# One plain feature tile fewer in the second up product of a macaron layer: three plain tiles instead of four

## The chip, the cores and the metric

The kernel runs on one core of one Trainium2 chip. The metric is the device time of one execution in microseconds (us), lower is better. Engines are named as the profile names them: PE (TensorE, matrix products), PEld (its weight loads), DVE (VectorE), ACT (ScalarE), POOL (GpSimd), SP (SyncE, which issues most transfers; its queue is SPq).

## The reference

One layer on 512 tokens of 1024 channels, in float32:

```
x = x + 0.5 * swiglu_ffn(rmsnorm(x, ffn1_norm), w_gate1, w_up1, w_down1)
x = x + hybrid_mixer(rmsnorm(x, mix_norm), w_in, ...)
x = x + 0.5 * swiglu_ffn(rmsnorm(x, ffn2_norm), w_gate2, w_up2, w_down2)
x = rmsnorm(x, final_norm)
swiglu_ffn(x, g, u, d) = (silu(x @ g) * (x @ u)) @ d      # hidden width 2816
```

The mixer is an attention over eight heads beside a pooling mixer. The change touches the third line alone, and in it the two products `x @ g` and `x @ u`.

## The kernel before, in words

**Numbers.** Every float32 operand of a product is split into a high part that PE can take (`hi`, made by ACT with a copy that rounds) and the rest (`lo`, made by DVE with a subtraction). A product then is three matrix instructions: high by high, high by low, low by high. `mm3` issues them, on lines 187, 188 and 189.

**The up product** (`ffn_up`, called once for each of the two feed-forward blocks). The 2816 hidden features are 22 tiles of 128. A tile needs its gate and its up column block, each 1024 x 128, against the 512 tokens. A tile is computed in one of two ways.

- *Plain*: 2 blocks x 8 pieces of the contraction x 3 instructions = 48 matrix instructions of 128x512. Weights: two transfers `raw<-in_wA_dram` (line 180), each split by ACT (L131, CAST) and DVE (L132).
- *Seven products*: contraction, tokens, and the pair gate/up are each halved, and the 2x2x2 block product is made with seven half-size products instead of eight (a Strassen-Winograd scheme). That is 7 x 4 pieces x 3 = 84 matrix instructions of 128x256. The order of the seven, by the activation operand: A11, S3, S2, A22, S1, A12, S4. Weights of the seven come as four parts: `11` (one block, 512 columns), `13` and `24` (sums made by DVE on lines 489, 495, 496) and `22`. ACT rounds each (L466), DVE makes the low part (L471). Below, "the low part of 24" is the L471 row that writes `parts<-wsum` with the 24 sum; product 3 (S2) is the first that reads it.

`PLAIN` gives the number of plain tiles of each block. With the second block's value of 4, the stage runs in this order:

1. Tiles 0 and 1 together, "the first group": 96 instructions into four accumulators (`first`). The norm of the tokens is finished in the middle of it, and only then is its row `rb` known.
2. Plain tiles 2 to plain - 2, each with its two blocks one after the other (line 514). For 4, this is tile 2.
3. Plain tile plain - 1, "the transition tile" (line 526), its two blocks interleaved piece by piece, so that the 16 normalized token buffers (`h`) come free one pair after another. Here ACT and DVE put the halved operands of the token side into those buffers (`ha`), and the first weights of the seven products are made.
4. Tiles plain to 21 by seven products (line 570), the order of PE, DVE and ACT written out by hand.

The token side of the seven products is a list of 19 steps, `norm.blocks` (line 337): eight scalings by the norm (L354), four sums of 128x1024 (L360), and seven splits: `xa` twice (S3 and S2, L134/L135), `sa` (S4), and four of two halves each, `ha` (A11, A22, S1, A12). The list `todo` holds them; `piece(n)` issues the next n:

```
for n, f in enumerate(down.order[2 : plain - 1], 2):     # 514
    for j in range(2):
        ... piece(4)                                     # 522
    down.make_sums(evacuate(f, *banks))
piece(len(todo) - 4)                                     # 524
...
for k in range(KD):                                      # 530, transition tile
    ... k == 1, 3, 5: piece()
high24(plain); low24(plain)                              # 546
down.make_sums(evacuate(f, *banks))
piece()
```

A plain tile is finished by `evacuate`: DVE multiplies the gate by `rb` (L413), ACT takes silu (L415), DVE multiplies again (L417) and multiplies with the up accumulator (L716); every second tile adds two short sums (L723, L724). In steps 1 to 3 a scheduler of the program's own decides the order on PE, DVE and ACT when the program is built; only SP keeps the written order. All engines then work through their own list in order.

Accumulators rotate through four `mm` banks and four `a` banks. Weight parts rotate through four places (three in `parts`, one in `whi`/`wlo`). `make_sums` lets POOL start the sums of the down weights; one call belongs to each tile from 2 on.

Of the kernel before, what the change touches and what calls it, by code (L numbers as in the profile page):

```python
# [34 lines left out]
RAW = 2  # L35
HILO = 3
SHIFT = 16
PLAIN = (5, 4)
PROBS = 3
EARLY = 8  # L40

# [14 lines left out]
def layer(  # L56
# [140 lines left out]
    def residual_tiles():  # L197
        pairs = [xpool.tile([P, 2 * S], F32, tag=f"x{k}", name=name("x")) for k in range(KD // 2)]
        x_pairs[:] = pairs
        return [pairs[k // 2][:, k % 2 * S : (k % 2 + 1) * S] for k in range(KD)]  # L200
# [651 lines left out]
    with tc.tile_pool(name="act1", bufs=1, reuse_waits="tile") as apool, ExitStack() as in_order:  # L852
        down1.begin(apool)
        ffn_up(n1, wA1, down1, False, in_order, PLAIN[0])
        x[:] = residual_tiles()
# [891 lines left out]
    with tc.tile_pool(name="act2", bufs=1, reuse_waits="tile") as apool, ExitStack() as in_order:  # L1747
        down2.begin(apool)

        ffn_up(n3, wA2, down2, True, in_order, PLAIN[1], (6, 7))  # L1750
        xt, gb = [None] * (2 * NT), [None] * 2
# [243 lines left out]
```

## Time and profile before

| what | value |
|---|---|
| median of 3 runs | 831.91 us (831.65 to 832.68) |
| the profiled execution's own time | 833.59 us |
| its span in the trace | 831.5 us |
| PE busy | 819.8 us (99%) |
| DVE busy | 715.0 us (86%) |
| ACT busy | 499.9 us (60%) |
| POOL busy | 147.2 us (18%) |

In a row of the timeline the columns are start, duration (us), engine, line, operation, output<-input, shape, count, and in square brackets the time the engine sat idle before it and what ended that. A PE row's duration overlaps the next row, so the pace of PE is read from the distance of two starts. Durations of DVE and ACT rows overlap the next by some 0.1 us too. A windows row gives, for a stretch, its length and the busy time of each engine.

### The profile page before, as it was taken

Reading aid. Unit: us, or ns where it says so; the run is one execution under the profiler, and the core shown is the slowest. Engines: PE = TensorE matmul, PEld = TensorE weight load, DVE = VectorE, ACT = ScalarE, POOL = GpSimd, SP = SyncE. Lnnn points to the kernel's source line nnn. Section 1 sums busy time; section 2 is a strip of 40 time slices with the busy share of each in tenths; the row PEclk is TensorE's granted clock in tenths of the full one; section 3 lists DMA queues with packets and bytes.
Section 4 is the critical chain, followed back from the end, with each engine's and each line's share of the span. In section 5 each row is a group of like instructions: output and inputs, shape, how many; then the busy total and the mean of one; then the engine's idle time right before and its main releaser. Section 6 shows DMA issues by size and latency. Waiting matters only on the chain.

```text
span 831.5 us, 15009 instructions
## 1 busy us (share of the span) xinstructions
PE 819.8 (99%) x5730; PEld 755.6 (91%) x5730; DVE 715.0 (86%) x1123; ACT 499.9 (60%) x854; POOL 147.2 (18%) x234
## 2 busy tenths in 40 slices
PE   9999999999999999999999999999999999999996
PEld 7889999999999999878878888899999999988885
DVE  7899999899987987678699688989999999977896
ACT  8346555666656665549659545465665555756573
POOL 0023212222310000334033063111111011100010
PEclk9999999999999999999999999999999999999998
DMA  8266989879998674999411267255666576859632
GB/s 282 73 203 204 239 221 260 205 198 235 253 303 280 194 225 140 240 308 242 173 52 52 82 156 213 68 108 204 160 181 158 148 206 158 275 195 317 202 115 102
DMA packets 73704, 158.56 MB, mean 191 GB/s; under 512 B 6545, under 2 KB 31649, under 8 KB 73249
## 3 DMA queue, kind: packets, MB, share of 16 engines
q1 hardware_dynamic: 49664, 109.09, 39.0%
q0 software_dynamic: 23680, 48.24, 27.6%
q8 instruction: 45, 0.74, 0.4%
q10 hardware_dynamic: 288, 0.27, 0.1%
q14 instruction: 27, 0.21, 0.1%
HBM read 153.38 MB, written 50.34 MB: 245 GB/s over the span
## 4 chain that ended last, share of the span: by engine, by line
PE 94%; DVE 2%; DMA 2%; ACT 1%; issue 0%; SPq 0%; DVEq 0%; ACTq 0%
PE mm L187 21%; PE mm L189 21%; PE mm L188 21%; PE a L187 9%; PE a L188 9%; PE a L189 9%; DMA raw<-in_wQK_dram 1%; PE a L1588 1%; DMA raw<-in_wA_dram 1%; PE mm L1499 1%; PE mm L1563 1%; PE a L1563 0%; PE mm L1588 0%; DVE t L1332 0%; DVE parts L1109 0%
## 5 line engine op out<-in xcount | busy, mean ns | idle before, releaser
L131 ACT CAST parts<-raw 128x1024 fp32r<-128x1024 f32 (+2 forms) x77 | 74.0, 969 | 63.0 <-PE mm L188 27.2
L560 ACT ACTIVATE t<-mm 128x256 f32<-128x256 f32 x105 | 40.3, 384 | 115.3 <-PE mm L189 112.5
L132 DVE TENSOR_TENSOR parts<-raw,parts 128x1024 fp32r<-128x1024 f32 (+2 forms) x77 | 85.7, 1121 | 20.7 <-ACT parts L131 17.5
L187 PE MATMUL mm<-ha,parts 128*128 128x256 f32 x280 | 77.4, 277 | 0.0
L189 PE MATMUL mm<-ha,parts 128*128 128x256 f32 x280 | 77.4, 277 | 0.0
L188 PE MATMUL mm<-ha,parts 128*128 128x256 f32 x280 | 77.4, 276 | 0.0
L706 POOL DMA_DIRECT2D wsum<-in_wB_dram x72 | 71.5, 1167 | 28.1 <-DMA wsum<-wsum 14.5
L704 POOL COPY mark<-t 128x1 f32<-128x1 f32 x40 | 16.1, 402 | 338.2 <-DVE t L604 249.7
L471 DVE TENSOR_TENSOR parts<-wsum,parts 128x1024 fp32r<-128x1024 f32 x53 | 64.6, 1219 | 5.8 <-PE mm L189 4.0
L466 ACT CAST parts<-wsum 128x1024 fp32r<-128x1024 f32 x53 | 53.9, 1049 | 0.4 <-DVE wsum L496 0.2
L187 PE MATMUL mm<-hhi,parts 128*128 128x512 f32 x136 | 53.3, 396 | 0.6 <-ACT parts L131 0.5
L189 PE MATMUL mm<-hhi,parts 128*128 128x512 f32 x136 | 53.2, 394 | 0.0
L188 PE MATMUL mm<-hlo,parts 128*128 128x512 f32 x136 | 52.9, 390 | 0.0
L187 PEld LDWEIGHTS mm<-ha,parts 128*128 128x128 f32 x280 | 52.6, 188 | 0.1
L188 PEld LDWEIGHTS mm<-ha,parts 128*128 128x128 f32 x280 | 52.6, 188 | 0.1
L189 PEld LDWEIGHTS mm<-ha,parts 128*128 128x128 f32 x280 | 52.6, 188 | 0.0
L132 DVE TENSOR_TENSOR ah<-acts,ah 128x512 fp32r<-128x512 f32 (+1 forms) x72 | 47.2, 663 | 5.1 <-ACT ah L131 5.1
L131 ACT CAST ah<-acts 128x512 fp32r<-128x512 f32 (+1 forms) x72 | 40.9, 580 | 9.9 <-PE mm L188 7.6
L471 DVE TENSOR_TENSOR parts<-raw,parts 128x512 fp32r<-128x512 f32 (+1 forms) x52 | 43.5, 860 | 0.0
L489 DVE TENSOR_TENSOR wsum<-raw 128x1024 f32<-128x1024 f32 x35 | 42.7, 1219 | 0.0
L1109 DVE TENSOR_TENSOR parts<-raw,parts 128x1024 fp32r<-128x1024 f32 x24 | 30.3, 1266 | 12.8 <-ACT parts L1104 12.7
L466 ACT CAST parts<-raw 128x512 fp32r<-128x512 f32 (+1 forms) x52 | 39.3, 755 | 2.0 <-DMA raw<-in_wA_dram 1.4
(340 smaller groups left out, 3050.4 us busy)
## 6 DMA issues: line engine op xcount, KB each, us to landing
raw<-in_wA_dram SPq DMA_DIRECT2D x87, 512.0 KB, 4.9
wsum<-in_wB_dram POOLq DMA_DIRECT2D x60, 512.0 KB, 7.7
raw<-wsum SPq DMA_DIRECT2D x36, 512.0 KB, 4.7
raw<-in_wB_dram SPq DMA_DIRECT2D x30, 512.0 KB, 5.1
wsum<-wsum POOLq DMA_DIRECT2D x20, 512.0 KB, 5.3
x<-in_xT_dram SPq DMA_DIRECT2D x16, 256.0 KB, 9.0
raw<-in_wQK_dram SPq DMA_DIRECT2D x8, 512.0 KB, 5.7
wsum<-in_wB_dram POOLq DMA_DIRECT2D x12, 256.0 KB, 6.2
```

The lines of the kernel that those rows point to most:

```text
L131: nc.scalar.copy(hi, src)
L132: nc.vector.tensor_tensor(lo, src, hi.bitcast(F32), op=ALU.subtract)
L187: nc.tensor.matmul(acc, a[0], b[0], start=start, stop=False, **more)
L188: nc.tensor.matmul(acc, a[0], b[1], start=False, stop=False, **more)
L189: nc.tensor.matmul(acc, a[1], b[0], start=False, stop=stop, **more)
L466: nc.scalar.copy(hi, src)
L471: nc.vector.tensor_tensor(lo, src, hi.bitcast(F32), op=ALU.subtract)
L489: nc.vector.tensor_tensor(z, raw[:, : 2 * S], raw[:, S : 3 * S], op=ALU.add)
L560: nc.scalar.activation(dst, src, AF.Copy, scale=scale)
L704: nc.gpsimd.tensor_copy(mark[:, 0:1], after[:, 0:1])
L706: nc.gpsimd.dma_start(self.rows(i, g), self.rows(self.terms[i][at], g), **(dict(accum_op=ALU.add) if at else {}),)
L1109: nc.vector.tensor_tensor(lo, buf["raw", i], hi.bitcast(F32), op=ALU.subtract)
```

## The change

The number of plain tiles of the second up product goes from 4 to 3:

```
-PLAIN = (5, 4)
+PLAIN = (5, 3)
```

`ffn_up` is called with `plain = 3`. The loop on line 514 is empty; tile 2 becomes the transition tile, and tile 3 is made of seven products. `piece(len(todo) - 4)` now issues 15 of the 19 steps right after the first group, where it used to find 11 left and issued 7. In the rows below names carry their buffer numbers: `aside` is the room of scaled tokens and their sums, `raw` a weight as it came, `wsum` a sum of weights.

On DVE, at the end of the first group (difference of the two orders; `raw_6269` and `raw_6302` are the weights of the old tile 2, `raw_6363` the first of the old transition tile, `raw_6293` and `raw_6297` those of the new one):

```order
-L132 TENSOR_TENSOR parts<-raw_6269,parts 128x1024
 L354 SCALAR_TENSOR_TENSOR aside_6264<-x_2854,gain_sb,rb_6212 128x512 x2
 L354 SCALAR_TENSOR_TENSOR aside_6264<-x_2855,gain_sb,rb_6212 128x512 x2
-L132 TENSOR_TENSOR parts<-raw_6302,parts 128x1024
 L354 SCALAR_TENSOR_TENSOR aside_6265<-x_2856,gain_sb,rb_6212 128x512 x2
 L354 SCALAR_TENSOR_TENSOR aside_6265<-x_2857,gain_sb,rb_6212 128x512 x2
+L132 TENSOR_TENSOR parts<-raw_6293,parts 128x1024
 L360 TENSOR_TENSOR aside_6266<-aside_6264,aside_6265 128x1024
-L132 TENSOR_TENSOR parts<-raw_6363,parts 128x1024
+L132 TENSOR_TENSOR parts<-raw_6297,parts 128x1024
 L360 TENSOR_TENSOR aside_6264<-aside_6266,aside_6264 128x1024
```

All eight scalings now stand together, and behind them both weight splits are already those of the transition tile.

On DVE, around the low part of 24, before (`wsum_6439` is the 24 sum, `mm_6373` and `mm_6374` the accumulators of the transition tile):

```order
L132 TENSOR_TENSOR ha_6479<-aside_6265,ha_6478 128x512
L413 TENSOR_TENSOR t_6464<-mm_6373,rb_6212 128x512
L471 TENSOR_TENSOR parts<-wsum_6439,parts 128x1024
L417 TENSOR_TENSOR t_6466<-t_6466,rb_6212 128x512
L132 TENSOR_TENSOR ha_6483<-aside_6265,ha_6482 128x512
L716 TENSOR_TENSOR acts_6093<-mm_6374,t_6466 128x2x256
```

and in the changed kernel (`wsum_6369` is the 24 sum, `wlo_6346` the low part of 13, `mm_6301` and `mm_6302` the accumulators):

```order
L471 TENSOR_TENSOR wlo_6346<-wsum_6343,whi_6345 128x1024
L496 TENSOR_TENSOR wsum_6369<-wsum_6369,raw_6303 128x512
L132 TENSOR_TENSOR ha_6373<-aside_6266,ha_6372 128x512
L413 TENSOR_TENSOR t_6394<-mm_6301,rb_6212 128x512
L132 TENSOR_TENSOR ha_6377<-aside_6266,ha_6376 128x512
L471 TENSOR_TENSOR parts<-wsum_6369,parts 128x1024
L417 TENSOR_TENSOR t_6396<-t_6396,rb_6212 128x512
L132 TENSOR_TENSOR ha_6407<-aside_6265,ha_6406 128x512
L716 TENSOR_TENSOR acts_6093<-mm_6302,t_6396 128x2x256
```

Two of the eight `ha` rows stand behind the low part of 24 instead of one, and the low part of 13 has moved close ahead of it.

On ACT, the rounding of the weights for the first tile of seven products, in the changed kernel (`parts<-raw_6303` is 22, `parts<-wsum_6369` is 24; the L560 row copies the sum of product 1 out of its accumulator):

```order
L466 CAST whi_6345<-wsum_6343 128x1024
L131 CAST ha_6372<-aside_6266 128x512
L466 CAST parts<-raw_6303 128x1024
L131 CAST ha_6376<-aside_6266 128x512
L466 CAST parts<-wsum_6369 128x1024
L415 ACTIVATE t_6396<-t_6394 128x512
L131 CAST ha_6406<-aside_6265 128x512
L560 ACTIVATE t_6422<-mm_6419 128x256
```

Before, 24 stood ahead of 22 in this list; now 22 is ahead, and behind 24 come the silu of the transition tile, one more `ha`, and then the copy.

On PE, at the start of the transition tile, in the changed kernel (`mm_6301` is its gate accumulator, `mm_6302` its up accumulator, in the bank that held the up block of tile 0):

```order
L189 MATMUL mm_6301<-hhi_5902,parts 128x512
L187 MATMUL mm_6301<-hhi_5916,parts 128x512
L188 MATMUL mm_6301<-hlo_5917,parts 128x512
L189 MATMUL mm_6301<-hhi_5916,parts 128x512
L187 MATMUL mm_6302<-hhi_5887,parts 128x512
L188 MATMUL mm_6302<-hlo_5888,parts 128x512
```

The scheduler put the gate's first three pieces (nine instructions) ahead of the up block's first; the code alternates them one piece at a time.

## The prediction

> **What bounds the kernel now.** I read the page first: how much of the chain that ended last is PE.
>
> ```profile
> span 831.5 us, 15009 instructions
> ...
> PE 94%; DVE 2%; DMA 2%; ACT 1%; issue 0%; SPq 0%; DVEq 0%; ACTq 0%
> ```
>
> PE is the end's chain nearly everywhere, so a PE instruction less is time less, as long as the operands of the next ones are there. That is a question of the stage, so I read the stage in windows: plain tile 2, the transition tile, the first tile of seven products, and the 17 that follow.
>
> ```profile
> 524.34:535.22 10.88, 10.88 (x49) 9.02 (x49) 10.88 (x16) 4.61 (x7) 1.68 (x1) 1.00 0.00 1
> 535.22:546.10 10.88, 10.88 (x49) 9.02 (x48) 8.77 (x13) 5.85 (x9) 1.99 (x2) 1.00 0.42 122
> 546.10:555.72 9.62, 9.62 (x85) 9.62 (x84) 9.55 (x15) 6.19 (x12) 1.99 (x4) 1.00 0.52 112
> ...
> 555.72:717.50 161.78, 161.78 (x1430) 161.78 (x1429) 149.65 (x211) 96.44 (x175) 22.05 (x39) 1.00 0.65 181
> ```
>
> The first busy number is PE, the third DVE, the fourth ACT. PE is busy all through, at full clock (1.00). A plain tile takes 10.88 us, a tile of seven products 161.78 / 17 = 9.52 us, the first of them 9.62. But DVE is busy through all of plain tile 2 (10.88 of 10.88) and through nearly all of the first product tile (9.55 of 9.62). Later DVE needs 149.65 / 17 = 8.80 us of each 9.52. **So PE sets the time, and DVE, which makes the operands, is only just ahead of it at the place where the change works.**
>
> **What the change removes from PE.** The pace of PE, from the distance of starts:
>
> ```profile
> 524.34 0.39 PE L187 MATMUL mm<-hhi,parts 128*128 128x512 f32 x1
> 524.57 0.39 PE L188 MATMUL mm<-hlo,parts 128*128 128x512 f32 x1
> ...
> 526.38 0.39 PE L187 MATMUL mm<-hhi,parts 128*128 128x512 f32 x1
> ...
> 546.10 0.28 PE L187 MATMUL mm<-ha,parts 128*128 128x256 f32 x1
> 546.22 0.28 PE L188 MATMUL mm<-ha,parts 128*128 128x256 f32 x1
> ...
> 548.84 0.35 PE L187 MATMUL mm<-xa,parts 128*128 128x256 f32 x1
> 549.03 0.28 PE L188 MATMUL mm<-xa,parts 128*128 128x256 f32 x1
> ```
>
> A 128x512 instruction takes (526.38 - 524.34) / 9 = 0.227 us; 48 of them are 10.88. A 128x256 one takes 9.52 / 84 = 0.113; 84 are 9.52. The gain on PE is 1.36 us. The first product tile lost 0.10 us, most of it at 548.84, where product 3 waited; counted apart, since that tile is replaced too: 1.36 + 0.10 = **1.46 us to gain, if PE never waits**. That is 0.18% of the time: small, so waits decide.
>
> The Trainium skill ("TensorE: Matmul & The Clock Gate", section on the back-to-back issue gap) says that in a real kernel the spacing is set by the matrix product and the weight load together, and gives 81 ns at 128 columns and 131 ns at 512. As an estimate from that page, 48 x 131 ns = 6.3 us against 84 x (81 to 131) ns = 6.8 to 11.0 us would make the smaller products the dearer ones by 0.5 to 4.7 us. The starts quoted above do not agree: 227 ns and 113 ns, in proportion to the columns.
>
> **What the change takes away as cover.** Plain tile 2 gave DVE 10.88 us while PE needed little from it. In the changed kernel PE starts the transition tile at 524.34 and the first product tile at 535.22 instead of 546.10. DVE loses with tile 2 only two weight splits and one tile's evacuation; the 19 token steps stay. So I add up DVE's list up to the low part of 24, in the changed order, with durations of this trace as distances of starts:
>
> ```profile
> 509.99 0.59 ACT L331 COPY rb<-a 128x512 f32<-128x512 f32 x1 [0.48 <-PE a L329]
> ...
> 511.47 2.73 DVE L354 SCALAR_TENSOR_TENSOR aside<-x,gain_sb,rb 128x512 f32<-128x512 f32 x4
> 514.52 1.23 DVE L132 TENSOR_TENSOR parts<-raw,parts 128x1024 fp32r<-128x1024 f32 x1 [0.31 <-ACT parts L131]
> 515.66 2.73 DVE L354 SCALAR_TENSOR_TENSOR aside<-x,gain_sb,rb 128x512 f32<-128x512 f32 x4
> ...
> 521.11 1.22 DVE L360 TENSOR_TENSOR aside<-aside,aside 128x1024 f32<-128x1024 f32 x1
> 522.24 1.22 DVE L360 TENSOR_TENSOR aside<-aside 128x1024 f32<-128x1024 f32 x1
> 523.38 0.69 DVE L413 TENSOR_TENSOR t<-mm,rb 128x512 f32<-128x512 f32 x1
> 523.98 1.22 DVE L135 SCALAR_TENSOR_TENSOR xa<-aside,xa 128x1024 fp32r<-128x1024 f32 x1
> ...
> 530.98 0.42 DVE L723 TENSOR_TENSOR acts<-acts 128x256 f32<-128x256 f32 x1
> 531.32 1.22 DVE L132 TENSOR_TENSOR sa<-aside,sa 128x1024 fp32r<-128x1024 f32 x1
> ...
> 546.58 1.22 DVE L471 TENSOR_TENSOR parts<-wsum,parts 128x1024 fp32r<-128x1024 f32 x1
> ```
>
> The prices: a scaling 0.66 (four last 2.73 and the last alone about 0.75), a step of 1024 elements 1.14 (514.52 to 515.66; 1.13 from 521.11 to 522.24), a step of 512 elements 0.60 (523.38 to 523.98), a short sum 0.34 (530.98 to 531.32). DVE can start when `rb` is there, 509.99 + 0.59 = 510.6. Then stand, in the changed order:
>
> - eight scalings, 5.3; two weight splits, 2.3; four sums, 4.5: 12.1 us, to 522.7;
> - two `xa` and one `sa`, 3.4; the evacuation of tiles 0 and 1, six times 0.60 and two short sums, 4.3: to 530.4;
> - low part of 11, 0.6; the sums of 13 and 24, 1.14 + 0.6 + 0.6; low part of 13, 1.14: 4.1, to 534.5;
> - six `ha` halves, 3.6, and the first multiplication of the transition tile's evacuation, 0.6: to 538.7.
>
> So the low part of 24 runs from 538.7 and, with its 1.22, ends at **539.95**. I see no row in this list for which DVE would have to stand still: each input is ready some tenths before its turn. PE wants the part in the third instruction of product 3: 535.22 + 26 x 0.113 = 538.2. **PE waits there 1.8 us.** It was not so before: there the row started at 546.58 and was done at 547.80, one us ahead of product 3.
>
> ACT says the same by another way. Product 3 adds to the accumulator of product 1, so ACT must have copied product 1 out first (L560). Its rows before:
>
> ```profile
> 545.44 1.05 ACT L466 CAST parts<-wsum 128x1024 fp32r<-128x1024 f32 x1
> 546.39 0.62 ACT L131 CAST ha<-aside 128x512 fp32r<-128x512 f32 x1
> 546.91 0.63 ACT L415 ACTIVATE t<-t 128x512 f32<-128x512 f32 x1
> ...
> 548.38 0.37 ACT L560 ACTIVATE t<-mm 128x256 f32<-128x256 f32 x1
> ```
>
> The copy ended at 548.75 and product 3 began its wait-free run right after, at 548.84. Now the rounding of 22 stands ahead of that of 24. It needs the place that the transition tile's up block leaves at its end, 535.3; 0.95 for it, 0.52 for an `ha`, 0.95 for 24 bring ACT to 537.7; the silu waits for DVE's 538.1 row and ends its turn near 538.75, one more `ha` 0.5, the copy 0.37: 539.7. Product 3 would start at 539.7 instead of 537.94, **1.75 us late**. The two waits lie beside each other, so they cost 1.8 us once, not twice.
>
> **The next tiles.** DVE is behind now, and its list goes on. Further prices of the hand-written order:
>
> ```profile
> 551.92 1.22 DVE L489 TENSOR_TENSOR wsum<-raw 128x1024 f32<-128x1024 f32 x1
> 553.17 0.69 DVE L495 TENSOR_TENSOR wsum<-wsum,raw 128x512 f32<-128x512 f32 x1
> 553.90 0.69 DVE L496 TENSOR_TENSOR wsum<-wsum,raw 128x512 f32<-128x512 f32 x1
> 554.51 0.42 DVE L604 TENSOR_TENSOR t<-a,t 128x256 f32<-128x256 f32 x1
> ```
>
> From the start of the low part of 24 (538.7): itself 1.14, four rows of 0.60, 22's low part 1.14, 11's 0.60, the sums 1.25 + 0.73 + 0.61, two short rows 0.68 make 8.55, so the second tile's low part of 13 starts at 547.3 and ends at 548.5. PE begins that tile at 535.22 + 9.52 + 1.8 = 546.5 and wants the part 14 instructions later, at 548.1: a wait of 0.4. The low part of 24 then ends at 547.3 + 1.14 + 0.34 + 1.22 = 549.97, wanted at 549.9: 0.1. In the third tile the same sum gives the part of 13 at 557.5, wanted at 558.15; from there DVE's 0.7 us of air in each tile keeps it ahead.
>
> **The start of the transition tile** is at the edge too. Its up accumulator takes the bank of tile 0's up block, which DVE frees with an L716 row; by the list above that row starts at 525.7 and ends near 526.4. PE has nine gate instructions first and wants the bank at 526.38 (the third start quoted for PE). I count 0.05 us. The weights themselves are ready by 519.5, by the same list.
>
> **What is only moved.** The transfers of the first seven-product weights go out earlier; each takes 2.9 to 7.2 us and has more than that before its use. POOL's calls for the down sums stay 20, one a tile. The four places of the weight parts change roles by two, in the same cycle. I count nothing for these, with some tenths either way as the range.
>
> ```profile
> L180 SPq DMA_DIRECT2D raw<-in_wA_dram x21: 327/328/524, 1.2 to 509.8; - x21
> ...
> DMA to landing us min/median/max: 2.9/4.2/7.2
> ```
>
> **The sum.** Gained 1.46; lost 0.05 + 1.8 + 0.4 + 0.1 = 2.35, less rounding 2.3. Net **+0.8 us**. Against its own execution (833.59, the span of 831.5 and 2.1 around it) that is 834.4; that execution stood 1.7 above the median of 831.91, so the forecast against the median is **832.7 us**, +0.1%. A measurement of this kernel tells about 0.2%, 1.7 us, from no change.
>
> **The rivals.**
>
> Of the first rival the profile has one row to weigh, DVE's `ha` rows of the old kernel from 511.47 to 547.9:
>
> ```profile
> L132 DVE TENSOR_TENSOR ha<-aside,ha 128x512 fp32r<-128x512 f32 x7 | 4.8, 689 | 2.1 <-ACT ha L131 1.3 <-PE mm L188 0.7
> ```
>
> - *No wait appears.* If the low part of 24 were issued by 537.0 and the copy of product 1 done by 537.9, the whole 1.46 would stay: 830.45. For it: DVE does have idle slots in the old transition tile (8.77 of 10.88), so its list is not always tight. Against it: those slots (2.1 us) are waits for `ha`, whose room PE frees piece by piece, and the sum above holds no slot to squeeze; 1.75 us would have to be wrong in it. Chance 0.09. It stays inside 0.2%.
> - *The evacuation comes late at the start of the transition tile, and nothing takes that back.* Place: the up block's first instruction, at 526.38. The price is one for one, since ACT's chain to the copy of product 1 starts from the end of the transition tile: it keeps its 1.75 us however late that end is. The point from which it decides is 0.85 us: from there the total is 0.8 + 0.85 = 1.65, slower by 0.2%. What could do it: on ACT the rounding of 11 now stands ahead of the `xa` roundings. It waits for a transfer sent about 509.8 behind the others, landing by 517.0 if it takes the longest 7.2, and ACT is wanted for `xa` from 520.6. So 3.6 us of margin speak against it; small delays of 0.02 us in each of DVE's 40 rows speak for it. Typical result +2.3: 834.2. Chance 0.13.
> - *Half-size products are paced by their weight loads.* At 0.227 us for each of 84, the tile would be 19.0 us, and the time 831.91 + 8.2 + 0.8 = 840.9. The product tiles of this trace run at 0.113. Chance 0.01.
> - *The change does not do what it says.* The order shows 36 more PE instructions, 84 - 48. Excluded.
>
> **How the numbers follow.** Forecast 0.77, its own range 831.5 to 833.7: 0.8 us from delays that I did not see, as much from overlaps that I did not count, and the spread of the three runs. The no-wait case ends at 830.45, the late case about 834.2. Leaving out less than 2 in 10: 831.0 to 834.2. Faster than 830.25 needs more than the whole gain: 0.02. Slower than 833.55 is most of the late case and the upper edge of the forecast: 0.16. Within: 0.82.
>
> **What would show it.** In the changed profile: PE's idle time before product 3's third instruction (or its first) in the first product tile, 1.7 to 1.9 us, released by DVE L471 or ACT L560; 0.3 to 0.5 in the second tile at the low part of 13; nothing from the fourth tile on, which then runs at 9.52; DVE without idle time from 510.6 to 540. Wrong would be: PE's wait at another place, above all at 526.4 or 535.2, or waits past the third tile, or a changed pace in the down product behind.

## The result, and the profile after

The changed kernel takes **833.64 us** (median of 20 runs, 832.29 to 837.03). The kernel before, run beside it, takes 832.59 (20 runs, 831.62 to 834.31). The ratio is **1.0016, 95% interval 1.0009 to 1.0022**: about a microsecond slower. The forecast was +0.8 us: 832.7 against 831.91, the median of three runs that was known then. With twenty runs that median is 832.59, so it is the difference that is to be compared, +1.05 us.

The page of the changed kernel:

```profile
span 835.0 us, 15097 instructions
...
PE 820.9 (98%) x5766; PEld 757.8 (91%) x5766; DVE 719.0 (86%) x1129; ACT 503.1 (60%) x861; POOL 145.1 (17%) x234
...
PE 85%; DVE 6%; DMA 5%; issue 2%; ACT 1%; SPq 1%; DVEq 0%; ACTq 0%
```

The span is 3.5 us longer than before, more than the medians say; the profiled execution, 837.03 us, is the slowest of the twenty. So the first question is where in the span the difference lies. I cut it by starts of PE rows. The **stretch** below runs from the first product of the second block (`hhi,parts`) to the first instruction of the down product behind it (`parts,ah`). It holds all that the change touches.

| | before | after |
|---|---|---|
| first product of the second block | 500.77 | 503.35 |
| its plain part, to the first 128x256 instruction | 45.33 | 34.44 |
| its seven-product part, to the first down product | 171.46 | 183.28 |
| **stretch** | **216.79** | **217.72** |
| down product, to the last row of PE | 105.68 | 105.69 |

The stretch costs **+0.93 us**. Behind it nothing changed. The 2.58 us ahead of it lie in code that is the same in both kernels; the last experiment shows what they are. Rows of the changed kernel are therefore 2.57 or 2.58 us late against those of before, and "on the clock of before" means with 2.57 taken off.

The stretch in windows, cut at the first instruction of each tile: transition tile, first and second tile of seven products, third, and the rest (length, then busy time and rows of PE, PEld, DVE, ACT, POOL, then the granted clock of PE):

```profile
526.91:537.79 10.88, 10.88 (x49) 9.01 (x48) 10.88 (x18) 4.78 (x8) 0.00 (x0) 1.00 0.01 4
537.79:549.26 11.47, 9.91 (x85) 9.71 (x84) 11.40 (x17) 7.17 (x12) 1.40 (x2) 1.00 0.32 55
549.26:559.23 9.97, 9.92 (x87) 9.72 (x86) 9.87 (x16) 6.41 (x11) 1.62 (x4) 1.00 0.89 225
559.23:568.75 9.52, 9.52 (x87) 9.52 (x86) 9.01 (x13) 5.74 (x12) 1.78 (x3) 1.00 0.77 185
568.75:721.07 152.32, 152.32 (x1347) 152.32 (x1345) 140.75 (x200) 90.55 (x164) 20.41 (x36) 1.00 0.65 177
```

PE is idle in two of these rows only: it works 9.91 of 11.47 us in the first product tile, 9.92 of 9.97 in the second. A PE row lasts longer than its pace, so busy time hides short waits; the lengths show them. Against the 9.52 us of every later tile the first lost 1.95 and the second 0.45, together 2.40 us. DVE, the third busy number, is full in the transition tile and all but full in the first product tile. The gaps themselves, in the timeline of PE:

```profile
540.42 0.28 PE L189 MATMUL a<-xa,wlo 128*128 128x256 f32 x1
542.25 0.38 PE L187 MATMUL mm<-xa,parts 128*128 128x256 f32 x1 [1.56 <-ACT t L560]
...
550.74 0.28 PE L188 MATMUL a<-xa,whi 128*128 128x256 f32 x1
551.07 0.39 PE L189 MATMUL a<-xa,wlo 128*128 128x256 f32 x1
```

At a pace of 0.113 from start to start, product 3 of the first product tile begins 1.72 us late, and two instructions close behind lose 0.11 and 0.06 more. In the second tile the low part of 13 costs 0.22 + 0.11, product 3 another 0.06. That is 2.28 of the 2.40 us; the rest are starts a little wider apart than 0.113, and no other gap in the stretch is new.

What DVE did there, with no idle time in brackets on any row:

```profile
538.86 0.68 DVE L496 TENSOR_TENSOR wsum<-wsum,raw 128x512 f32<-128x512 f32 x1
539.47 0.68 DVE L132 TENSOR_TENSOR ha<-aside,ha 128x512 fp32r<-128x512 f32 x1
540.07 0.68 DVE L413 TENSOR_TENSOR t<-mm,rb 128x512 f32<-128x512 f32 x1
540.67 0.68 DVE L132 TENSOR_TENSOR ha<-aside,ha 128x512 fp32r<-128x512 f32 x1
541.27 1.21 DVE L471 TENSOR_TENSOR parts<-wsum,parts 128x1024 fp32r<-128x1024 f32 x1
```

and ACT:

```profile
539.58 1.05 ACT L466 CAST parts<-wsum 128x1024 fp32r<-128x1024 f32 x1 [0.20 <-DVE wsum L496]
540.78 0.63 ACT L415 ACTIVATE t<-t 128x512 f32<-128x512 f32 x1 [0.15 <-DVE t L413]
541.32 0.60 ACT L131 CAST ha<-aside 128x512 fp32r<-128x512 f32 x1
541.83 0.37 ACT L560 ACTIVATE t<-mm 128x256 f32<-128x256 f32 x1
```

The low part of 24 starts at 541.27, on the clock of before at 538.70, and is there at 542.48. The copy of product 1 is done at 542.20, and PE goes on at 542.25. The trace names the copy, but ACT itself waits for DVE twice on the way to it (L496, L413). That is still a reading of one trace: the copy alone, the order on ACT, or DVE's list could each be the cause, and they end within 0.3 us of each other. The experiments take them apart.

### The profile page after: what moved, and what is told of

Its sections match the earlier page's. It is cut to its first block, busy times and chain, and to the rows that moved or that the text cites. A ratio compares the mean times of both kernels' runs of the same rounds, so it can differ in the third digit from the quotient of the medians.

```text
span 835.0 us, 15097 instructions
## 1 busy us (share of the span) xinstructions
PE 820.9 (98%) x5766; PEld 757.8 (91%) x5766; DVE 719.0 (86%) x1129; ACT 503.1 (60%) x861; POOL 145.1 (17%) x234
## 4 chain that ended last, share of the span: by engine, by line
PE 85%; DVE 6%; DMA 5%; issue 2%; ACT 1%; SPq 1%; DVEq 0%; ACTq 0%
PE mm L187 19%; PE mm L188 18%; PE mm L189 18%; PE a L187 9%; PE a L188 9%; PE a L189 9%; DMA raw<-in_wQK_dram 2%; DMA t<-ext_d 1%; DMA raw<-in_wV_dram 1%; DVE parts L1109 1%; PE a L1588 1%; DMA raw<-in_wA_dram 1%; PE mm L1499 1%; PE mm L1563 1%; DVE aside L354 1%
## 5 line engine op out<-in xcount | busy, mean ns | idle before, releaser
L560 ACT ACTIVATE t<-mm 128x256 f32<-128x256 f32 x108 | 41.5, 384 | 117.6 <-PE mm L189 114.6
L131 ACT CAST parts<-raw 128x1024 fp32r<-128x1024 f32 (+2 forms) x74 | 70.9, 967 | 56.6 <-PE mm L188 23.0
L132 DVE TENSOR_TENSOR parts<-raw,parts 128x1024 fp32r<-128x1024 f32 (+2 forms) x74 | 82.1, 1116 | 15.7 <-ACT parts L131 15.1
L187 PE MATMUL mm<-ha,parts 128*128 128x256 f32 x288 | 79.5, 276 | 0.0
L189 PE MATMUL mm<-ha,parts 128*128 128x256 f32 x288 | 79.5, 276 | 0.0
L188 PE MATMUL mm<-ha,parts 128*128 128x256 f32 x288 | 79.5, 276 | 0.0
L471 DVE TENSOR_TENSOR parts<-raw,parts 128x512 fp32r<-128x512 f32 x72 | 65.8, 950 | 0.6 <-ACT parts L466 0.6
L466 ACT CAST parts<-raw 128x512 fp32r<-128x512 f32 x72 | 59.7, 829 | 5.2 <-DMA raw<-in_wA_dram 2.5
L187 PEld LDWEIGHTS mm<-ha,parts 128*128 128x128 f32 x288 | 54.1, 188 | 0.1
L188 PEld LDWEIGHTS mm<-ha,parts 128*128 128x128 f32 x288 | 54.1, 188 | 0.1
L189 PEld LDWEIGHTS mm<-ha,parts 128*128 128x128 f32 x288 | 54.1, 188 | 0.0
L471 DVE TENSOR_TENSOR wlo<-wsum,whi 128x1024 fp32r<-128x1024 f32 x36 | 44.1, 1224 | 10.3 <-PE mm L189 7.9
L187 PE MATMUL mm<-hhi,parts 128*128 128x512 f32 x128 | 50.6, 400 | 0.2 <-ACT parts L131 0.2
L189 PE MATMUL mm<-hhi,parts 128*128 128x512 f32 x128 | 50.0, 394 | 0.0
L188 PE MATMUL mm<-hlo,parts 128*128 128x512 f32 x128 | 49.7, 390 | 0.0
L471 DVE TENSOR_TENSOR parts<-wsum,parts 128x1024 fp32r<-128x1024 f32 x36 | 43.7, 1215 | 0.0
```

The source lines that it names most:

```text
L131: nc.scalar.copy(hi, src)
L132: nc.vector.tensor_tensor(lo, src, hi.bitcast(F32), op=ALU.subtract)
L187: nc.tensor.matmul(acc, a[0], b[0], start=start, stop=False, **more)
L188: nc.tensor.matmul(acc, a[0], b[1], start=False, stop=False, **more)
L189: nc.tensor.matmul(acc, a[1], b[0], start=False, stop=stop, **more)
L466: nc.scalar.copy(hi, src)
```

## The experiments

The theory is that of the prediction: DVE's list decides when product 3 may go. The rivals are ACT's copy, and ACT's order (22 rounded ahead of 24). Every kernel is the changed one with the edit shown.

**One: the copy no longer matters (e1).** Products 3, 5 and 7 of the first product tile go to an empty bank; product 1 is thereby left out of that tile's later sums.

```
-                product(acc, cut(w24, 0, S), S2, False)
+                acc = abank()[:, :HT] if n == plain == 3 else acc; product(acc, cut(w24, 0, S), S2, n == plain == 3)
```

> Changed kernel, but in the first tile of seven products (tile 3 of the second block) products 3, 5 and 7 are summed in a spare bank that begins empty, so that product 3 need not wait for ACT's copy of product 1 (L560). Left out of the computation: product 1 in the sums behind it, for this one tile. The list of DVE is the same. Theory (DVE is behind; its low part of 24 ends 2.5 us after product 3 could start): PE's wait stays, 1.6 to 1.8 us, and moves from the first to the third instruction of product 3, released by DVE L471; the stretch from the first hhi product of the second block to its first down product stays 217.7 us within 0.15. Rival (ACT's copy alone holds PE, 24 is ready earlier): the wait falls under 0.5 us and the stretch to 216.5 or less.

Measured: 832.62 us in one run, stretch 217.82. PE's timeline, then DVE's:

```profile
538.01 0.39 PE L189 MATMUL a<-xa,parts 128*128 128x256 f32 x1 [1.36 <-DVE parts L471]
```

```profile
536.73 1.23 DVE L471 TENSOR_TENSOR parts<-wsum,parts 128x1024 fp32r<-128x1024 f32 x1
```

The wait moved by two instructions, to the first that reads the low part of 24, and kept its size (1.52 beyond the pace there). The stretch stayed. Taking the copy away gains nothing, since DVE's row is as late as the copy. So the copy alone is not the cause.

**Two: 22 rounded behind the copy (e6).**

```
-                high(n, (n, 22), raws[n][:, 2 * S :])
-                low((n, 22))
-                w22 = w[n, 22][:2]
+                first3 = n == plain == 3
+                if not first3: high(n, (n, 22), raws[n][:, 2 * S :]); low((n, 22))
...
+                if first3: high(n, (n, 22), raws[n][:, 2 * S :]); low((n, 22))
+                w22 = w[n, 22][:2]
```

> Changed kernel, but ACT's rounding of 22 for the first product tile stands behind the copy of product 1 instead of ahead of the rounding of 24; 24 is ahead of 22 as in the kernel before. DVE's list is unchanged up to the low part of 24. Theory (DVE's list sets it; silu, and with it the copy behind it, wait for DVE's L413 row): PE's wait at product 3 stays 1.6 to 1.8 us, the stretch stays 217.7 within 0.15 us. Rival (the turned order of ACT made the wait): copy and 24 are ready 0.9 us earlier and the wait falls to 0.9 us or less, stretch 216.9 or less.

Measured: 833.96 us in one run, stretch 218.09. ACT, then PE:

```profile
536.11 1.05 ACT L466 CAST parts<-wsum 128x1024 fp32r<-128x1024 f32 x1 [1.48 <-DVE wsum L496]
...
538.28 0.38 ACT L560 ACTIVATE t<-mm 128x256 f32<-128x256 f32 x1
```

```profile
538.71 0.39 PE L187 MATMUL mm<-xa,parts 128*128 128x256 f32 x1 [1.57 <-ACT t L560]
...
540.97 0.39 PE L187 MATMUL a<-ha,parts 128*128 128x256 f32 x1 [0.57 <-ACT t L560]
```

With 22 out of the way ACT stands idle 1.48 us for DVE's 24 sum, and product 3 is 1.73 us late, as before. ACT's order is not the cause. I missed one thing: the second copy, which product 4 needs, now stands behind 22's rounding and costs 0.74 us. The waits of the second tile went (0.39), so the stretch is 0.37 longer than in the changed kernel; the expected 217.7 was wrong.

**Three and four: more on DVE (e11, e13).** Two of the eight scalings, then one, are issued twice, far ahead of the place.

```
-                nc.vector.scalar_tensor_tensor(
+                for _ in range(2 if self.which == 2 and k > 5 else 1): nc.vector.scalar_tensor_tensor(
```

> Two of the eight scalings of the second block are issued twice (same result): 1.2 to 1.3 us more on VectorE ahead of all its rows of the transition. Theory (VectorE's list sets the wait): low 24 comes that much later, and since VectorE has no idle time there the waits of PE in products 2 to 4 of the first product tile grow by as much, from 1.9 to about 3.1 us; nothing new at the transition's start; stretch 218.9 us, within 0.2. Rival (ScalarE's copies or the weights' parts in the pool set it, and VectorE has time to spare): stretch 217.7, waits as they were.

> One of the eight scalings of the second block issued twice (same result), half of what e11 added: low 24 comes 0.6 us later than in the changed kernel, so the gap ahead of product 3 is about 2.3 us long, between the 1.85 us after which the granted clock stayed at 1.00 and the 2.7 us after which it fell to 0.50. If only the length of the wait counts: extra wait 1.9 + 0.6, stretch 218.3, within 0.2. If the clock falls behind this gap too: stretch 219.5 or more.

Measured, one run each: 836.25 us and stretch 220.22 with two rows more; 836.81 and 219.60 with one. (The times of single runs are not compared: the one with one row more stood still for 1.32 us at 96 us, in another stage.) On the clock of before (each kernel set by its own first product of the block) the low part of 24 starts at 540.06 and 539.39 instead of 538.70, so 1.36 and 0.69 us later for 1.2 to 1.3 and 0.6 put in. PE's timeline of the kernel with one row more:

```profile
538.66 0.28 PE L189 MATMUL a<-xa,wlo 128*128 128x256 f32 x1
540.77 0.38 PE L187 MATMUL mm<-xa,parts 128*128 128x256 f32 x1 [1.83 <-ACT t L560]
...
541.33 0.41 PE L187 MATMUL mm<-xa,parts 128*128 128x256 f32 x1
541.54 0.41 PE L188 MATMUL mm<-xa,parts 128*128 128x256 f32 x1
```

The theory holds: the wait grows with DVE's list, to 2.0 us at product 3 and 0.39 at product 2 with one row, to 2.58 and 0.44 with two. But the stretch grew by 1.88 and 2.50, more than the rows. From 541.33 on PE's starts are 0.21 apart instead of 0.113. Windows of the gap and of the 2.6 us behind it show why, first for the changed kernel, then with one row more, then with two:

```profile
540.42:542.25 1.83, 0.28 (x3) 0.08 (x1) 1.83 (x3) 1.68 (x5) 0.00 (x0) 1.00 0.00 0
542.25:544.90 2.65, 2.65 (x22) 2.65 (x23) 2.65 (x6) 1.64 (x4) 1.40 (x2) 1.00 0.00 0
```

```profile
538.66:540.77 2.11, 0.28 (x4) 0.08 (x2) 2.11 (x3) 1.96 (x5) 0.00 (x0) 1.00 0.00 0
540.77:543.40 2.63, 2.63 (x13) 2.63 (x14) 2.63 (x6) 1.24 (x3) 1.40 (x2) 0.58 0.00 0
```

```profile
537.77:540.46 2.69, 0.28 (x3) 0.07 (x1) 2.69 (x4) 2.52 (x5) 0.00 (x0) 0.94 0.00 0
540.46:543.10 2.64, 2.64 (x12) 2.64 (x13) 2.64 (x6) 1.25 (x3) 1.41 (x2) 0.50 0.00 0
```

Behind a gap of 1.83 us from start to start (1.56 idle) the granted clock stayed at 1.00; behind 2.11 (1.83 idle) it was 0.58, behind 2.69 (2.41 idle) it was 0.50, where 12 or 13 matrix instructions ran instead of 22. So the 218.9 expected for two rows, which counted the wait alone, was too low; with one row it was the second of the two cases that came, 219.5 or more. The second price of the longer gap is some 1.6 us more.

**Five: the other direction (e5).** `PLAIN = (5, 5)`, one plain tile more than before.

> The other direction: five plain tiles in the second product instead of four (one half-size tile fewer than before). If a plain tile costs 1.36 us more on PE than one of half-size products, whatever stands beside it, and the wait exists only where three plain tiles leave VectorE too little time: stretch 216.79 + 1.36, less up to 0.1 for the old wait, 218.05 to 218.2; time 1.3 us above before, ratio 1.0016. Rival (half-size products cost more than their pace, so that less is lost by leaving them): stretch 217.5 or less, ratio 1.0008 or below.

Measured: 835.04 us (12 runs), ratio 1.0034 (1.0021 to 1.0047), stretch 218.40. The lengths of the parts, and of the product tiles from start to start:

| plain tiles | plain part | first product tile | second | each later one |
|---|---|---|---|---|
| 3 | 34.44 | 11.47 | 9.97 | 9.52 |
| 4 | 45.33 | 9.62 | 9.52 | 9.52 |
| 5 | 56.28 | 9.68 | 9.64 | 9.52 |

A plain tile more adds 10.89 and then 10.95 us to the plain part, and a product tile fewer takes away 9.52. That is 1.37 and 1.43 us for each tile exchanged, 1.40 on the mean, against 1.36 by the pace. The rival, that half-size products cost more than their pace, falls. The expected stretch was 0.2 short: the first two product tiles lose 0.28 us here, where at most 0.1 was reckoned with. The expected ratio of 1.0016 lies outside the interval: the stretch's +1.61 us explains 1.0019, and what the rest is stays open.

**Six: a hand-written order (e8).** The transition is written out by hand instead of left to the scheduler, the short sums of tile 1 are put off, and in the first product tile 22 is rounded behind the copy of product 1, as in e6:

```
+            step(10)
+            step(13)
+            high11(plain)
+            low11(plain)
+            sum13(plain)
+            z0 = gate(first[0])
...
+            step(17)
+            z2 = gate(banks[0])
+            high24(plain)
+            low24(plain)
...
+                if hand: high(n, (n, 22), raws[n][:, 2 * S :]); low((n, 22))
```

> Changed kernel with the order of PE, DVE and ACT from the first scaling to the end of the transition tile written by hand, the most urgent first; the two short sums of tile 1 (0.7 us of DVE) go to a later tile; otherwise the same work on the same engines. Theory (DVE has too much to do before the second product tile, in whatever order): PE's waits move to the start of the transition tile (about 1.3 us at the up block's bank) and to the second tile's 13 (0.2), about 1.6 us in all instead of 2.3; stretch 217.1 us (216.8 to 217.4), time 0.2 us above the kernel before. Rival (the scheduler's order is at fault): the waits all but vanish, stretch 215.6, time 1.3 us below the kernel before.

Measured: 834.0 us (10 runs), ratio 1.0018 (1.0009 to 1.0027), stretch 218.60. Product 3 waits 0.71 us in place of 1.89, but product 4 now 0.89, and the transition tile's start, which was free, 1.04 and a little later 0.45. That is 3.1 us where 1.6 were expected. The wait at the start:

```profile
523.94 0.47 PE L187 MATMUL mm<-hhi,parts 128*128 128x512 f32 x1 [0.80 <-DVE t L526]
```

(L526 is L413 here.) DVE did 11's low part and the 13 sum ahead of the evacuation that frees the bank. So PE came to product 3 some 1.6 us later than in the changed kernel (plain part 36.06 us against 34.44), and the shorter wait there is no gain. The wait at product 4 is the one that e6 made by moving 22. This order pays at one end what it takes from the other; that no order could do better, it does not show.

**Seven: two sums to POOL (e9).** The same, and two of the four 128x1024 sums of the token side run on POOL.

```
-                (add, a21, a11, a21, ALU.add),
+                (add, a21, a11, a21, ALU.add, nc.gpsimd if self.which == 2 else None),
...
-                (add, s4, s2, a12, ALU.subtract),
+                (add, s4, s2, a12, ALU.subtract, nc.gpsimd if self.which == 2 else None),
```

> The same hand-written order, and two of the four sums of 128x1024 of the token side (the one for S3 and the one for S4, 2.3 us of DVE) made by POOL. Theory (DVE's amount of work is what is lacking): PE's waits in the transition and the first two product tiles fall under 0.4 us; stretch 215.4 to 215.8 us; time 1.0 to 1.4 us below the kernel before (ratio 0.9983 to 0.9988). Rival 1 (what POOL does beside DVE slows DVE's rows, or POOL is too slow for S3): rows of DVE at 512 to 526 us longer than 1.22, waits over 1 us, no gain over the hand-written order without POOL. Rival 2 (something behind the stage takes the gain back): stretch as said, time unchanged.

Measured: 836.39 us (6 runs), ratio 1.0053 (1.0038 to 1.0068), stretch 220.76. POOL, then DVE, then PE:

```profile
516.59 6.10 POOL L360 TENSOR_TENSOR aside<-aside 128x1024 f32<-128x1024 f32 x1 [4.01 <-DVE aside L360]
522.65 3.34 POOL L360 TENSOR_TENSOR aside<-aside,aside 128x1024 f32<-128x1024 f32 x1
```

```profile
519.21 1.22 DVE L490 TENSOR_TENSOR wsum<-raw 128x1024 f32<-128x1024 f32 x1
...
521.25 2.52 DVE L135 SCALAR_TENSOR_TENSOR xa<-aside,xa 128x1024 fp32r<-128x1024 f32 x1
523.70 2.85 DVE L533 TENSOR_TENSOR t<-t,rb 128x512 f32<-128x512 f32 x1
527.00 0.69 DVE L804 TENSOR_TENSOR acts<-mm,t 128x512 f32<-128x512 f32 x1 [0.46 <-DVE t L533]
```

```profile
527.84 0.47 PE L187 MATMUL mm<-hhi,parts 128*128 128x512 f32 x1 [3.15 <-DVE acts L804]
```

DVE does such a sum in 1.22 us. POOL took 6.10 and 3.34, and beside it two DVE rows took 2.52 and 2.85 instead of 1.22 and 0.69. The bank came late, PE stood 3.15 us and then ran at a lower clock (0.59 on the mean of the next 3.7 us). This is rival 1. At product 3 no wait was left, but PE came there 5.1 us later than in the changed kernel (plain part 39.51 us against 34.44), so this run does not tell what a shorter list of DVE is worth.

**Eight and nine: fewer rows ahead, by putting them off (e10, e12).** The evacuation of the transition tile, the short sums of tile 1 and the split of `sa` move behind the low part of 24; the copies go ahead of 22's rounding; a second `a` bank serves the first product tile. In e10 the evacuation's first steps stand at the head of the second product tile:

```
+            low13(plain)
+            sum24(plain)
+            low11(plain)
...
+            high24(plain)
+            low24(plain)
+            step(14)
+            step(18)
+
+            def gate_later():
+                late.append(gate(banks[0]))
+                silu(late[0])
```

> A hand-written order of the second product's transition, with what product 3 of the first product tile waits for brought forward: VectorE gets the low part of 24 ahead of the evacuation of the transition tile, of one of the sums' roundings and of the short sums of tile 1 (the evacuation follows in the second and third product tiles, the short sums in the fifth and seventh), ScalarE's copies stand ahead of 22's rounding. Same result as the reference. Theory (VectorE's list sets the wait): counted by the rows of the changed kernel, low 24 starts about 2.5 us earlier than there, so the wait of 1.7 us at product 3 goes; waits of PE in the transition and in the first two product tiles together at most 0.4 us; stretch from the first product of the second block to the first down product 215.4 to 215.9 us (217.72 in the changed kernel, 216.79 before); time about 1.1 us below the kernel before, ratio 0.9985. Rival (the wait only moves, as in e8, because the rows put back collide with the product tiles' own): stretch 217 or more, ratio 1.000 or above.

Measured: 836.11 us (7 runs), ratio 1.0035 (1.0022 to 1.0048), stretch 220.22. Product 3 of the first product tile lost 0.17 us, so the wait in question is gone. But in the second tile, ACT and then PE:

```profile
550.45 0.63 ACT L532 ACTIVATE t<-t 128x512 f32<-128x512 f32 x1 [2.79 <-DVE t L528]
550.99 0.37 ACT L654 ACTIVATE t<-a 128x256 f32<-128x256 f32 x1
```

```profile
551.40 0.58 PE L187 MATMUL a<-ha,parts 128*128 128x256 f32 x1 [2.43 <-ACT t L654]
```

I had put the silu (L532) ahead of the copy (L654) that frees product 4's bank. Its input is late on DVE's list, ACT takes its rows in order, and PE waits: the same trap as in the changed kernel, one tile on. The clock fell behind this gap too. The rival, a wait that only moves, had come. e12 puts the two steps near that tile's end and gives its `up_lo` an `a` bank:

```
+                if n == 4 and plain == 3:
+                    gate_later()
...
+                if n == 4 and plain == 3:
+                    silu_later()
```

> e10 with its new wait taken away: there the Silu of the transition tile stood on ScalarE ahead of the copy that frees product 4's bank in the second product tile, and its input came late on VectorE's list. Here both of the evacuation's first steps stand behind that copy, near the tile's end, and the second tile's up_lo gets another bank too. Same result. Theory (VectorE's list and what stands behind it on ScalarE set all waits): PE waits in the transition and the first two product tiles at most 0.6 us together, granted clock 1.00 throughout, stretch 215.9 to 216.4 us (before 216.79, changed kernel 217.72), time about 0.7 us below the kernel before, ratio 0.9985 to 0.9995. Rival (a product tile's own rows leave VectorE no room for the moved ones, so the wait turns up in the second or third tile again): stretch 217 or more, ratio 1.000 or above.

Measured: 831.95 us (11 runs), ratio **0.9993 (0.9984 to 1.0002)**, stretch **216.44**, the shortest of all. Its windows, from the transition tile to the fourth product tile:

```profile
524.40:535.27 10.87, 10.87 (x48) 8.76 (x48) 10.28 (x16) 6.58 (x11) 0.00 (x0) 1.00 0.00 1
535.27:545.14 9.87, 9.87 (x86) 9.76 (x84) 9.80 (x14) 6.35 (x12) 0.00 (x0) 1.00 0.29 94
545.14:554.98 9.84, 9.84 (x86) 9.75 (x85) 9.74 (x15) 6.43 (x12) 2.42 (x4) 1.00 0.52 147
554.98:564.78 9.80, 9.80 (x87) 9.61 (x85) 9.70 (x15) 5.90 (x12) 1.89 (x4) 1.00 0.89 189
564.78:574.30 9.52, 9.52 (x87) 9.52 (x85) 9.30 (x15) 5.57 (x11) 1.32 (x4) 1.00 0.55 168
```

The first three product tiles take 9.80 to 9.87 us instead of 9.52, so 0.95 us remains there in small gaps, with DVE busy for nearly all of the three tiles; the transition tile loses 0.14. For the transition and the first two tiles together that is 0.8 where 0.6 was expected. Of the 2.4 us that the changed kernel loses, 1.3 are regained. e10 and e12 change several things at once (rows put off, copies ahead, one more bank), so they show that the wait goes when DVE's list up to the low part of 24 is shorter, but not what each part is worth. The stretch is 0.35 us below before, the time not measurably so: the interval reaches past 1.

**Ten: the 2.6 us ahead of the stretch (e14, e15).** The two kernels once more, unchanged.

> The changed kernel itself once more, for what its first profile had ahead of the stretch: there the second block's first product started at 503.35 us, 2.6 us later than in the kernel before, in a stage whose code is the same in both; in the eight experiments it started between 498.8 and 501.2. If that was one execution's chance, the start now lies between 498.8 and 501.5, the stretch is 217.7 again, within 0.15, with the gap ahead of product 3 at 1.8 us and the clock at 1.00 behind it, and the profiled time is about 834. If it belongs to the changed kernel, the start is 503 again.

> The kernel before once more, as a second profile of it: start of the second block's first product between 498.8 and 501.5, stretch 216.8, within 0.1, no gap ahead of product 3.

Measured: after 834.12 us (12 runs), ratio 1.0018 (1.0007 to 1.0029), first product at 499.47, stretch 217.80, product 3 again 1.73 us late; before 833.94 us in one run, first product at 501.15, stretch 216.80. So the stretch repeats to 0.1 us and the start does not. Most of what the first profile of the changed kernel lost there lies in the mixer, in the list of waits (us in total, times, longest; before, then after):

```profile
PE mm L1499 <- DVE sm L1507: 0.7, 2, 0.5
```

```profile
PE mm L1499 <- DVE sm L1507: 2.7, 2, 2.4
```

In the second profile of the changed kernel PE does not wait there at all. The long wait had a second price: the granted clock stood at 0.50 for 3.41 us behind it (from 374.61). From 369 to 377 us PE fell back by 3.48 us against the kernel before, having been 0.84 ahead. It was that execution's chance, not the change.

Stretch and time agree over the timed kernels but e5, whose time rose by more than its stretch: +0.93 and +1.00 us of stretch for the changed kernel's two profiles went with ratios of 1.0016 and 1.0018, +1.81 (e8) with 1.0018, +3.43 (e10) with 1.0035, +3.97 (e9) with 1.0053, -0.35 (e12) with 0.9993.

## Why the prediction was right

- **The gain on PE**, 1.36 us a tile: right; 1.37 from four plain tiles to three, 1.40 on the mean by the kernels with 3 and 5.
- **The lost cover**: right in mechanism and size. DVE's list was summed to a start of the low part of 24 at 538.7; it started at 538.70, and no row of the list stood still. The wait at product 3 was given as 1.8 us and came as 1.72 + 0.11 + 0.06 = 1.89. e1, e6, e11 and e13 show the cause: it survives without the copy's dependence and without 22 ahead of 24, and moves with rows added to DVE.
- **"ACT says the same by another way"**: right. The copy was put at 539.7 and ended at 542.20 - 2.57 = 539.63. It was not a second cost: in e1 the wait only passed from the copy to DVE's row.
- **The second tile**: 0.4 at the low part of 13 and 0.1 at 24 predicted, 0.33 and 0.06 measured; nothing from the third on, as said.
- **The transition tile's start**: 0.05 predicted, nothing measured. It was at the edge: the row that frees the bank ended at 528.92 and PE used the bank at 528.95. In e8 and e9 this edge was crossed.
- **The sum**: +0.8 predicted, +0.93 and +1.00 in the stretch, +1.05 between medians. By its terms: lost 2.40 where 2.3 stood (2.35 before rounding), gained 10.89 - 9.52 + 0.10 = 1.47 where 1.46 stood, the old wait included. The prediction held 1.7 us to be the least that a measurement tells from no change; twenty runs of each kernel told 1.05.
- **What was counted as nothing**: the product tiles from the third on run at 9.52 us and the down product takes 105.69 us against 105.68, so the earlier transfers and POOL's calls cost nothing that shows. The same 9.52 answers the rival that half-size products are paced by their weight loads.
- **The no-wait rival** would have needed a low part of 24 by 537.0. e10 and e12 bring it to 537.15 by moving rows away, and the wait there shrinks to 0.2 us; the order that the scheduler made had no such room.
- **The late evacuation** did not come about, but its price was wrong in the text. I had it one for one. e9 shows a late bank at that very place: PE stood 3.15 us and lost speed behind it, so a long gap costs more than its length. Nor did the wait at product 3 keep its size behind a late start: 0.71 us were left in e8, none in e9, though with another order of the rows. The changed kernel stands near to the fall of the clock: its gap is 1.83 us from start to start, and at 2.11 the clock fell.

## What to carry to other kernels

When a stage is shortened on the engine that sets the time, add up the list of the engine that feeds it, row by row and in the new order, up to the first operand that is wanted; here that sum was right to 0.1 us and gave the sign. A wait that names one engine may end within tenths of another: take one away before believing it, and look at what stands in order ahead of the releasing row. Work that is put off must not put a late-fed row ahead of a copy that frees a bank.

## What the runs showed of the hardware

- **PE's clock falls behind a gap of less than 2 us.** In all thirteen traces the granted clock changes only at whole multiples of 3.413 us, counted from the first 1.00 that is recorded. In e13 it stays at 1.00 for 157 and 84 such periods, in the changed kernel's first profile for 108 and 133, and each fall to 0.50 between lasts one period. It fell behind the five periods in the course of a kernel with the most idle time of PE: 1.83 us (e13), 1.88 (e10), 2.06 (e11), 2.63 (the changed kernel's first profile, in the mixer) and 2.76 (e9). It did not fall behind 1.57 (e6), 1.56 (the changed kernel's second profile) or anything shorter. The period of e13's gap, the next and the one behind:

```profile
537.77:541.18 3.41, 1.58 (x13) 1.38 (x13) 3.41 (x6) 2.93 (x6) 0.00 (x0) 1.00 0.00 0
541.18:544.60 3.42, 3.42 (x18) 3.42 (x18) 3.42 (x6) 1.22 (x4) 1.40 (x2) 0.50 0.23 19
544.60:548.01 3.41, 3.41 (x31) 3.41 (x31) 3.34 (x6) 1.15 (x2) 0.00 (x0) 1.00 0.85 192
```

So where a gap lies seems to count as well as how long it is: the 1.56 us of the changed kernel's first profile were cut by a border into 1.16 and 0.39. That a gap above 1.83 us goes unpunished when it is cut that way, no run here shows. The Trainium skill (TensorE: Matmul & The Clock Gate, section on HAM oscillation) warns of idle gaps above about 3.4 us; in the runs here the clock had fallen behind 1.83 us.

- **POOL is no spare DVE.** A 128x1024 float32 sum took it 3.34 to 6.10 us by its rows against 1.22, and two DVE rows beside it took two and four times as long: 3.46 us lost on DVE, for two sums that would have taken it 2.3. The Trainium skill (SBUF — State Buffer, section on the two separate sides) says that the two engines hold a shared pair of ports by turns. The trace agrees with that in the rows that stretched, though three other DVE rows beside the first sum kept their usual time. The ends of the rows fit turns too. The last of those three, L490, ended at 520.43; POOL's sum ended 2.26 us later, and DVE's `xa` row 1.08 after that, at 523.77. POOL's second sum ended 2.22 us behind that, and DVE's next row 0.56 later. Read so, POOL works some 2.2 us on a sum and waits for its turn in the rest of its row; this is an estimate from these rows, and no run has POOL alone.
